# Conv-FFN epilogue in two parts, another order in the pool, first statistics on TensorE

## The chip, the core and the metric

The kernel runs on one core of a Trainium2 chip. The metric is device time in microseconds (us) of one execution; the time of a kernel is the median of its runs. One more execution was taken with the hardware profiler; all rows of the trace are from that one.

## What is computed

One inference step of a trunk of four layers. The input is 128 context tokens and 256 latent tokens, together T = 384 columns of width 1024. Each layer has a token mixer and a Conv-FFN, each behind an RMS norm with shift, scale and gate from the conditioning vector (adaLN):

```python
h = rms_norm(x, g_mix[i]) * (1 + sc1) + sh1
y = chunk_gmlp(h) | multi_pool(h) | attention(h)      # layers 0 and 3 | 1 | 2
x = x + gt1 * y
h = rms_norm(x, g_ffn[i]) * (1 + sc2) + sh2
a, u = jnp.split(h @ w_in, 2, axis=-1)                # 2 x 2816 columns
a = ap[:, :-2] * conv_w[0] + ap[:, 1:-1] * conv_w[1] + ap[:, 2:] * conv_w[2] + conv_b
x = x + gt2 * ((gelu(a) * u) @ w_out)
```

`multi_pool` takes, in four groups of 256 channels, the mean over a window of tokens minus the token itself, and multiplies by a 256 x 256 matrix per group.

## The kernel before

**Layout.** `x` stays in SBUF, transposed: 8 slices of 128 channels by 384 tokens. Every matmul of weights is done in three passes (`mm3`, `vmm`): a weight chunk is split into a rounded part `whi` (ScalarE, line 353) and a remainder `wlo` (VectorE, line 360), the activations likewise (`hh`, `hl`, or `gh`, `gl`), and whi x hi, wlo x hi and whi x lo are added up in PSUM.

**Weights.** All weight chunks (128 x 1024 fp32, 512 KB) stand in one list (`chunk_plan`) in the order of use. `load` issues their transfers on SyncE's queue, at most five ahead of the oldest chunk whose buffer is not free yet. `w_get` hands out the next chunk and splits up to three chunks ahead (four buffers each for `whi` and `wlo`), through `w_split`: first all `whi`, then what the caller gives as `mid`, then `wlo`; only then is the chunk's buffer free for the next transfer. Chunks named `ad` are adaLN weights. They are woven into the list between others (`weave`; `EDGES` says after how many chunks of a phase the first one comes, and how many stand behind the last), and each costs VectorE two products, line 395 (`junk`).

**Order.** Each engine runs its instructions in program order, and that order is written out by hand. So an instruction that waits holds up all that stands behind it on its engine.

**FFN** (`ffn`). The weights of f = 0 and 1 come first (four chunks, `fr`), with the statistics in their midst, then f = 2 to 21, two chunks each (`fi`; in the code kk = 0 and 1, here the halves of f). f fills two PSUM banks, `pa` and `pu`. The pool of banks `mm` has six; f = 3 uses two others. The first NR values of f (3, in layer 1: 4) run on activations that are not yet normed, and their epilogue multiplies by `rbs` first; meanwhile `norm` makes the normed ones. The epilogue of an f is in three parts: `epi_a` (only for f < NR: takes both banks into SBUF), `epi_b` (the convolution: `ab`, `ct`) and `epi_c` (GELU, times u: `gg`); `split_act` then makes `gh` and `gl`. In the first half of f come `epi_a` (as `mid`) and `epi_b` of f - 1 (in the beginning of f - 2), in the second half:

```python
gs = [epi_c(st, t) for st, t in zip(sts, ts)]
w = self.w_get("fi")
for st, g in zip(sts, gs):
    self.split_act(g, gh[st[0]], gl[st[0]])
```

At f = 5 the epilogues of 3 and 4 are done together. For f >= NR `epi_b` reads `pa` and `epi_c` reads `pu` in PSUM.

**Pool** (layer 1). For each of four groups g: `first(g)` multiplies by the group's matrix into two banks; `scaled(g)` takes them into SBUF with the norm's factor `r`; `second(g)` makes the means with the matrices of the windows, for two slices d, each with its residual and the preparation of the next norm (`aft`).

**Head.** `warm` runs matmuls on ones. `x` comes in four transfers. VectorE and ScalarE square and add it up, `first_stats` (in the middle of `a0_mm(0)`) has TensorE add over the channels. `a0_mm(d)` multiplies the conditioning vector with two chunks of adaLN weights for slice d, `a0_fin(d)` turns the result and adds the bias. `diag` and `spread` bring the norm's factor to all partitions, `put` writes the normed slice 0. Then `gmlp` runs over 8 slices k (chunks `gr`, passes of 6 matmuls, line 852), with `a0_fin(k + 1)` behind the first pass and `a0_mm(k + 2)` behind the second.

## Time and profile before

| | |
|---|---|
| median of 3 runs | 1771.77 us (1771.72 to 1775.01) |
| profiled execution | 1772.34 us |
| its span, first to last instruction | 1770.6 us |
| mean granted clock of TensorE | 0.999 |

A row of the trace gives a start and a length in us from the span's start, the engine (PE is TensorE, PEld its weight load, DVE VectorE, ACT ScalarE, SP SyncE), the line of the kernel, what is written from what, and in brackets how long the engine had been idle and what ended that. xN are N instructions put together. An fp32 matmul appears as two instructions.

### The profile page before, as it was taken

The page shows a single profiled execution, that of the slowest core. Times are in us where ns is not written, and L with a number is a line of the kernel's source. Part 1 is how long each engine was busy: PE and PEld are TensorE (multiplying, and loading weights), DVE is VectorE, ACT ScalarE, POOL GpSimd, SP SyncE. Part 2 cuts the span into 40 slices and gives each one's busy share as a digit, 9 for nine tenths or more (in the row PEclk, how much of TensorE's full clock was granted, in tenths as well). Part 3 has the DMA queues.
Part 4 walks back from the last instruction along what each step waited for, and adds up shares of the span by engine and source line. Part 5 has one row for each costly group of instructions (what it writes and reads, how often), then busy time and mean ns, then how long its engine had stood idle before and what let it go on. Part 6 is the DMA issues. An engine that isn't in the chain of part 4 may idle for free.

```text
span 1770.6 us, 26877 instructions
## 1 busy us (share of the span) xinstructions
PE 1748.9 (99%) x10282; PEld 1671.1 (94%) x10282; DVE 1347.4 (76%) x2309; ACT 885.5 (50%) x1661; POOL 3.4 (0%) x32
## 2 busy tenths in 40 slices
PE   9999999999999999999999999999999999999999
PEld 7799899999998999999778999999988999999999
DVE  6888778888986788886787788887775676876632
ACT  4644346444456654532568564553354444754521
POOL 0000000000000000000000000000000000000000
PEclk9999999999999999999999999999999999999999
DMA  9765654565662356566443336556645334354341
GB/s 338 281 220 167 230 196 139 195 199 188 232 219 106 108 190 202 185 226 208 175 150 132 119 132 200 191 173 202 196 166 192 119 132 155 118 180 147 133 155 54
DMA packets 87728, 312.03 MB, mean 176 GB/s; under 512 B 10478, under 2 KB 10990, under 8 KB 87344
## 3 DMA queue, kind: packets, MB, share of 16 engines
q1 hardware_dynamic: 87216, 309.91, 51.4%
q8 instruction: 80, 1.31, 0.3%
q0 software_dynamic: 96, 0.41, 0.1%
q14 instruction: 48, 0.39, 0.1%
q10 hardware_dynamic: 288, 0.01, 0.0%
HBM read 308.45 MB, written 1.84 MB: 175 GB/s over the span
## 4 chain that ended last, share of the span: by engine, by line
PE 79%; DVE 12%; ACT 5%; issue 3%; DMA 2%; ACTq 0%; DVEq 0%; SPq 0%
PE mm L678 60%; PE mm L852 6%; DVE wlo L360 4%; DVE junk L395 4%; ACT whi L353 2%; DMA wraw<-wts 2%; DVE ct L726 2%; PE adaT L678 2%; PE S L678 1%; PE psa L678 1%; PE mm L896 1%; PE S L1133 1%; PE adaT L852 1%; PE psa L852 1%; PE O L1353 0%
## 5 line engine op out<-in xcount | busy, mean ns | idle before, releaser
L678 PE MATMUL mm<-hb,whi 128*128 128x384 f32 (+1 forms) x3936 | 859.2, 337 | 0.0
L678 PEld LDWEIGHTS mm<-hb,whi 128*128 128x128 f32 x3936 | 698.2, 188 | 3.6 <-issue 1.2
L360 DVE TENSOR_TENSOR wlo<-wraw,whi 128x1024 fp32r<-128x1024 f32 (+2 forms) x390 | 466.0, 1201 | 211.7 <-ACT whi L353 211.2
L353 ACT ACTIVATE whi<-wraw 128x1024 fp32r<-128x1024 f32 (+2 forms) x390 | 399.6, 1034 | 252.2 <-PE mm L678 156.1
L678 PE MATMUL mm<-hb,wlo 128*128 128x384 f32 (+1 forms) x1968 | 504.5, 337 | 5.0 <-DVE wlo L360 4.9
L678 PEld LDWEIGHTS mm<-hb,wlo 128*128 128x128 f32 x1968 | 355.9, 188 | 7.8 <-DVE wlo L360 7.8
L395 DVE SCALAR_TENSOR_TENSOR junk<-wraw,condb 128x1024 bf16<-128x1024 f32 x288 | 351.9, 1222 | 7.9 <-ACT condb L1615 2.7
L735 ACT ACTIVATE gg<-ct 128x128 f32<-128x128 f32 (+1 forms) x150 | 46.4, 356 | 245.6 <-DVE ct L726 245.6
L678 PE MATMUL mm<-gh,wlo 128*128 128x384 f32 x448 | 123.3, 336 | 0.6 <-DVE wlo L360 0.6
L678 PE MATMUL mm<-gh,whi 128*128 128x384 f32 x448 | 123.3, 336 | 0.0
L678 PE MATMUL mm<-gl,whi 128*128 128x384 f32 x448 | 123.2, 336 | 0.0
L726 DVE SCALAR_TENSOR_TENSOR ct<-ab,par,ct 128x385 f32<-128x385 f32 x176 | 108.6, 619 | 6.2 <-ACT ct L724 2.5
L852 PE MATMUL mm<-whi,hb 128*128 128x512 f32 x320 | 87.2, 397 | 0.0
L613 ACT ACTIVATE hb<-x,A 128x128 fp32r<-128x128 f32 x96 | 42.5, 455 | 86.1 <-DVE x L468 80.4
L678 PEld LDWEIGHTS mm<-gh,wlo 128*128 128x128 f32 x448 | 81.7, 188 | 1.0 <-DVE wlo L360 1.0
L678 PEld LDWEIGHTS mm<-gh,whi 128*128 128x128 f32 x448 | 81.7, 188 | 0.1
L678 PEld LDWEIGHTS mm<-gl,whi 128*128 128x128 f32 x448 | 81.8, 188 | 0.0
L736 DVE TENSOR_TENSOR gg<-mm,gg 128x384 f32<-128x384 f32 x72 | 40.2, 558 | 47.2 <-ACT gg L735 46.5
L852 PEld LDWEIGHTS mm<-whi,hb 128*128 128x128 f32 x320 | 59.4, 187 | 17.2 <-issue 2.5
L724 ACT ACTIVATE ct<-ab,par 128x385 f32<-128x385 f32 x88 | 62.7, 713 | 3.4
L468 DVE SCALAR_TENSOR_TENSOR x<-mm,prm,x 128x128 f32<-128x128 f32 x92 | 33.6, 411 | 27.0 <-PE mm L678 27.0
L852 PE MATMUL mm<-wlo,hb 128*128 128x512 f32 x160 | 47.0, 399 | 0.0
(291 smaller groups left out, 1769.4 us busy)
## 6 DMA issues: line engine op xcount, KB each, us to landing
wraw<-wts SPq DMA_DIRECT2D x562, 512.0 KB, 3.9
wraw<-wts SPq DMA_DIRECT2D x12, 256.0 KB, 2.9
wraw<-wts SPq DMA_DIRECT2D x8, 384.0 KB, 4.3
x<-x SPq DMA_DIRECT2D x4, 384.0 KB, 4.5
mx<-mix SPq DMA_DIRECT2D x1, 1280.0 KB, 8.3
y<-x SPq DMA_DIRECT2D x3, 384.0 KB, 4.8
condb<-condb SPq DMA_DIRECT2D x1, 1024.0 KB, 6.5
ws<-a_w_s SPq DMA_DIRECT2D x2, 512.0 KB, 5.5
```

The lines of the kernel that those rows point to most:

```text
L353: nc.scalar.activation(hi[:, :n], t[:, :n], AF.Copy)
L360: nc.vector.tensor_tensor(out=lo[:, :n], in0=t[:, :n], in1=hi[:, :n].bitcast(F32), op=ALU.subtract)
L395: nc.vector.scalar_tensor_tensor(out=self.junk.bitcast(BF16), in0=w, scalar=1.0, in1=self.condb[:, c, :], op0=ALU.mult, op1=ALU.mult, accu ...
L468: nc.vector.scalar_tensor_tensor(out=x[:, d, t0:t1], in0=ps[:, t0:t1], scalar=self.prm[:, l, ty * 8 + d, c:c + 1], in1=x[:, d, t0:t1], op0 ...
L613: nc.scalar.activation(self.hh[:, d, t0:t1], self.x[:, d, t0:t1], AF.Copy, scale=A[:, d, c:c + 1])
L678: nc.tensor.matmul(o, w[:, c:c + nw], r, start=(first and p == 0), stop=(last and p == 2))
L724: nc.scalar.activation(t, ab[:, 1:T + 2], AF.Identity, scale=cw[1], bias=cb)
L726: nc.vector.scalar_tensor_tensor(out=t, in0=ab[:, i:i + T + 1], scalar=cw[i], in1=t, op0=ALU.mult, op1=ALU.add)
L735: nc.scalar.activation(g[:, t0:t1], t[:, t0 + c:t1 + c], GELU)
L736: nc.vector.tensor_tensor(out=g, in0=u, in1=g, op=ALU.mult)
L852: nc.tensor.matmul(ps[n][i], hs, w[p == 1][:, c:c + 512], start=(k == 0 and p == 0), stop=(k == 7 and p == 2))
L896: nc.tensor.matmul(ps[:, 128 * i:128 * i + 128], v[:, i, 128 * c:128 * c + 128], ws[:, c // 2, :], start=True, stop=True)
```

## The change

- FFN: the epilogue is one function, `epilogue`, called in both halves of every f. It gets the weights first (both `whi` and `wlo`, with `epi_a` between), then does `epi_c` and `split_act` for what is due, then `epi_b` for the new one, which is due in the next half. From f = 6 on `epi_b` of f - 1 stands in the second half of f, and its `epi_c` in the first half of f + 1. In f = 5 the epilogue of 3 begins in the first half and that of 4 in the second. In layer 1 `norm` takes 2 slices per half instead of 3.
- `EDGES`: in the FFN of layer 1 the first `ad` chunk comes after 12 chunks instead of 8.
- Pool: `first(3)` and `scaled(2)` stand ahead of `second(0)`, `scaled(3)` ahead of `second(1)`; `u` has four buffers instead of three.
- Head: each of the four pieces of `x` is squared (two by ScalarE, two by VectorE, the last in halves) and TensorE adds each up over the channels in its own columns; VectorE sums the five sets. `warm(0)` has 13 matmuls instead of 25, and `warm(1)` comes behind each piece. `a0_mm(0)` stands behind the statistics. The remainder of the first chunk stands behind the first `put`.

```diff
-EDGES = {(0, "gv"): (2, 1), (0, "go"): (5, 0), (3, "gv"): (5, 2), "fi": (8, 2), (3, "go"): (5, 2)}
+EDGES = {(0, "gv"): (2, 1), (0, "go"): (5, 0), (3, "gv"): (5, 2), (1, "fi"): (12, 2), "fi": (8, 2), (3, "go"): (5, 2)}
-WARM = (25, 3, 5)
+WARM = (13, 3, 5)
...
                     if k > stat_k + 1:
                         norm(2)
-            prev = [(0, b[0], b[1]), (1, b[2], b[3])]
+
+            prev, due = [(0, b[0], b[1]), (1, b[2], b[3])], []
+
+            def epilogue(todo, get):
+
+                sts = []
+                w = get(lambda: sts.extend([epi_a(*p) for p in todo]))
+                for st, t in due:
+                    self.split_act(epi_c(st, t), gh[st[0]], gl[st[0]])
+                due[:] = [(st, epi_b(st)) for st in sts]
+                return w
+
             for f in range(2, NF):
                 w0 = TE if f < NR[l] else T
                 pa, pu = (p()[:, :w0] for p in ((self.ps_bank, self.px_bank) if f == 3 else (self.bank, self.bank)))
-                now, prev = (prev, []) if f == 5 else (prev[:1], prev[1:])
                 for kk in range(2):
-                    if kk == 0:
-                        sts = []
-                        w = self.w_get("fi", mid=lambda: sts.extend([epi_a(*p) for p in now]))
-                        ts = [epi_b(st) for st in sts]
-                    else:
-                        gs = [epi_c(st, t) for st, t in zip(sts, ts)]
-                        w = self.w_get("fi")
-                        for st, g in zip(sts, gs):
-                            self.split_act(g, gh[st[0]], gl[st[0]])
+                    todo = [prev.pop(0)] if f < 6 and kk == 0 or f > 4 and kk == 1 else []
+                    w = epilogue(todo, lambda mid: self.w_get("fi", mid=mid))
                     if f < NR[l]:
-                        norm(3)
+                        norm(2 if NR[l] > 3 else 3)
                     for k4 in range(4):
                         k = 4 * kk + k4
                         r = (hh[:, k, :], hl[:, k, :]) if f < NR[l] else (nh[:, k, :], nl[:, k, :])
                         self.mm3([(pa, 256 * k4), (pu, 256 * k4 + 128)], w, r, k == 0, k == 7)
                 prev.append((f, pa, pu))
             assert next(steps, 0) == 0 and len(prev) == 1
-            sts = []
-            self.w_split(self.n_get + 2, lambda: sts.extend([epi_a(*p) for p in prev]))
-            g = epi_c(sts[0], epi_b(sts[0]))
-            self.split_act(g, gh[NF - 1], gl[NF - 1])
+            epilogue(prev, lambda mid: self.w_split(self.n_get + 2, mid))
+            epilogue([], lambda mid: None)
             self.use(1 - self.cur)
             res, after = follow()
             self.out_proj("fo", gh, gl, NF, l, 5, after, mid=self.sqrt_table, after_chunk=1)
...
             def scaled(g):
                 ps = us[g]
-                u = pp.tile([128, 3, 256], F32, tag="u", name="u", bufs=3)
+                u = pp.tile([128, 3, 256], F32, tag="u", name="u", bufs=4)
                 for i in range(3):
                     nc.scalar.activation(u[:, i, :], ps[i // 2][:, 256 * (i % 2):256 * (i % 2) + 256], AF.Copy,
                                          scale=r[:, i:i + 1])
...
             scaled(0)
             first(2)
             scaled(1)
+            first(3)
+            scaled(2)
             second(0)
-            scaled(2)
-            first(3)
+            scaled(3)
             second(1)
-            scaled(3)
             second(2)
             second(3)
             return res
...
         sel = self.cst[:, 512:514]
         rows = {}
-        def a0_mm(d, mid=None):
+        def a0_mm(d):
             if d >= KD:
                 return
             ps = self.ps_bank()[:, 0:256]
...
                     nc.tensor.matmul(ps[j:j + 32, :], self.cond[:, 4 * h + k4, :], w[:, 256 * k4:256 * k4 + 256],
                                      start=(h == 0), stop=(h == 1), skip_group_check=True)
                 self.free(i)
-                if mid is not None:
-                    mid()
-                    mid = None
             rows[d] = self.tmp.tile([128, 256], F32, tag="adarow", name="a0row", bufs=1)
             nc.vector.tensor_copy(rows[d], ps)
...
         nc.scalar.activation(self.cond[:, :, 0:2], cin, AF.Silu)
-        acc = self.new_acc()
         xf = self.x.rearrange("p k t -> p (k t)")
         with self.tc.tile_pool(name="start", bufs=1) as sp:
-            sum2 = sp.tile([128, 2 * T], F32, tag="sum2", name="sum2")
-            nc.vector.tensor_tensor(out=sum2, in0=xf[:, 0:2 * T], in1=xf[:, 0:2 * T], op=ALU.mult)
-            for d in range(2, KD, 2):
-                sq = sp.tile([128, 2 * T], F32, tag="sq2", name="sq2", bufs=3)
-                nc.scalar.activation(sq, xf[:, T * d:T * d + 2 * T], AF.Square)
-                nc.vector.tensor_tensor(out=sum2, in0=sum2, in1=sq, op=ALU.add)
-            nc.vector.tensor_tensor(out=acc, in0=sum2[:, 0:T], in1=sum2[:, T:2 * T], op=ALU.add)
+
+            cs = self.px.tile([128, 5, 3], F32, tag="px", name="cs")
+            for n in range(4):
+                sq = sp.tile([128, 2 * T], F32, tag="sq2", name="sq2", bufs=4)
+                t0 = 2 * T * n
+                if n in (1, 2):
+                    nc.scalar.activation(sq, xf[:, t0:t0 + 2 * T], AF.Square)
+                for c0, c1 in {0: [(0, 2 * T)], 3: [(0, T), (T, 2 * T)]}.get(n, ()):
+                    nc.vector.tensor_tensor(out=sq[:, c0:c1], in0=xf[:, t0 + c0:t0 + c1], in1=xf[:, t0 + c0:t0 + c1],
+                                            op=ALU.mult)
+                for g in ((0,), (1,)) if n == 3 else ((0, 1),):
+                    for i in range(3):
+                        for h in g:
+                            nc.tensor.matmul(cs[:, n + (n == 3 and h), i:i + 1],
+                                             sq[:, T * h + 128 * i:T * h + 128 * i + 128], self.ones[:, 0:1],
+                                             start=(h == g[0]), stop=(h == g[-1]), skip_group_check=True)
+                warm(1)
             self.sqrt_table()
-        r = []
-
-        def first_stats():
-            warm(1)
-            r.append(self.stats(acc))
-
-        a0_mm(0, first_stats)
+        m = self.tmp.tile([128, 3], F32, tag="ms", name="ms", bufs=1)
+        nc.vector.tensor_reduce(out=m, in_=cs.rearrange("p n i -> p i n"), op=ALU.add, axis=AX.X)
+        nc.vector.tensor_scalar(out=m, in0=m, scalar1=1.0 / D, scalar2=EPS, op0=ALU.mult, op1=ALU.add)
+        r = [self.rsqrt(m, [128, 3])]
+        a0_mm(0)
         warm(2)
-        R = []
-        self.w_split(1, lambda: R.append(self.diag(r[0])))
-        A = a0_fin(0)
-        rb = self.spread(R[0], self.bank)
         rbs = self.tmp.tile([128, T], F32, tag="acc", name="rb0", bufs=1)
-        self.put([0], lambda k: A, rb, *self.plain(0), 0)
-        nc.scalar.activation(rbs, rb, AF.Copy)
+
+        def first_put():
+            R = self.diag(r[0])
+            A = a0_fin(0)
+            rb = self.spread(R, self.bank)
+            self.put([0], lambda k: A, rb, *self.plain(0), 0)
+            nc.scalar.activation(rbs, rb, AF.Copy)
+
+        self.w_split(1, first_put)
         a0_mm(1)
         nc.sync.dma_start(self.cst[:, 0:512], a["cst"][:, 0:512])
```

## Rows read from the trace of the kernel before

**Rows 1.** The page: span, and busy time of the engines.

```profile
span 1770.6 us, 26877 instructions
...
PE 1748.9 (99%) x10282; PEld 1671.1 (94%) x10282; DVE 1347.4 (76%) x2309; ACT 885.5 (50%) x1661; POOL 3.4 (0%) x32
```

**Rows 2.** TensorE's waits: total us, times, longest.

```profile
PE mm L678 <- DVE wlo L360: 5.5, 8, 1.0
```

**Rows 3.** The chain that ended last: start us, us.

```profile
1035.05 245.52 PE mm L678 x1416
```

**Rows 4.** Warming matmuls alone in one stretch: PE busy (instructions), PEld, clock, DMA share, GB/s.

```profile
1.05:5.90 4.85, 4.85 (x22) 4.85 (x23) 1.00 0.82 266
```

**Rows 5.** The head in order of time: start us, us.

```profile
10.57 0.73 PE L536 MATMUL cs<-ones,acc 128*128 128x1 f32 x6
...
13.39 0.91 PE L551 MATMUL mm<-R,ones 128*128 128x384 f32 x2
...
15.25 0.64 PE L1545 MATMUL psa<-wraw,cond 128*32 128x256 f32 x8 [0.38 <-DMA wraw<-wts]
...
15.82 1.66 PE L852 MATMUL mm<-whi,hb 128*128 128x512 f32 x6
...
20.43 3.06 PE L852 MATMUL mm<-whi,hb 128*128 128x512 f32 x12
```

**Rows 6.** The page, DMA issues: count, KB, median us to landing.

```profile
wraw<-wts SPq DMA_DIRECT2D x562, 512.0 KB, 3.9
```

**Rows 7.** End of the pool and start of the FFN, in order of time.

```profile
550.92 0.42 PE L1045 MATMUL mm<-ms,us 66*128 66x384 f32 x1 [3.39 <-DVE us L1036]
...
553.01 0.74 DVE L1052 SCALAR_TENSOR_TENSOR x<-mm,pgs,x 128x128 f32<-128x128 f32 x2
...
555.87 0.87 PE L678 MATMUL mm<-hb,wlo 128*128 128x386 f32 x4
...
557.41 0.73 DVE L1052 SCALAR_TENSOR_TENSOR x<-mm,pgs,x 128x128 f32<-128x128 f32 x2
```

**Rows 8.** The same stretch: busy time (instructions) of PE, PEld, DVE, ACT, POOL; clock.

```profile
551.00:560.00 9.00, 9.00 (x42) 8.48 (x43) 7.85 (x22) 5.70 (x13) 0.27 (x6) 0.81 0.00 0
```

**Rows 9.** FFN of layer 0, in order of time: TensorE, then VectorE.

```profile
273.31 0.34 PE L678 MATMUL psa<-hb,whi 128*128 128x384 f32 x1
...
298.84 1.22 DVE L360 TENSOR_TENSOR wlo<-wraw,whi 128x1024 fp32r<-128x1024 f32 x1
299.98 1.22 DVE L395 SCALAR_TENSOR_TENSOR junk<-wraw,condb 128x1024 bf16<-128x1024 f32 x1
...
302.60 2.46 DVE L726 SCALAR_TENSOR_TENSOR ct<-ab,par,ct 128x385 f32<-128x385 f32 x4
...
305.75 0.56 DVE L736 TENSOR_TENSOR gg<-mm,gg 128x384 f32<-128x384 f32 x1 [0.22 <-ACT gg L735]
```

**Rows 10.** ScalarE groups in the FFN of layer 0: busy us, mean ns, idle before.

```profile
L724 ACT ACTIVATE ct<-ab,par 128x385 f32<-128x385 f32 x19 | 13.5, 713 | 0.6
...
L722 ACT ACTIVATE ab<-mm 128x128 f32<-128x128 f32 (+1 forms) x36 | 9.5, 314 | 0.0
L592 ACT ACTIVATE gh<-gg 128x384 fp32r<-128x384 f32 x12 | 6.0, 507 | 0.0
```

**Rows 11.** FFN of layer 1, in order of time: TensorE, VectorE.

```profile
590.38 0.51 PE L678 MATMUL mm<-hb,whi 128*128 128x384 f32 x2
...
613.43 1.22 DVE L360 TENSOR_TENSOR wlo<-wraw,whi 128x1024 fp32r<-128x1024 f32 x1
```

**Rows 12.** FFN of layer 2, in order of time: TensorE, VectorE.

```profile
1026.55 0.34 PE L678 MATMUL psa<-hb,whi 128*128 128x384 f32 x1
...
1052.27 1.22 DVE L360 TENSOR_TENSOR wlo<-wraw,whi 128x1024 fp32r<-128x1024 f32 x1
```

**Rows 13.** FFN of layer 3, in order of time: TensorE, VectorE.

```profile
1517.04 0.34 PE L678 MATMUL psa<-hb,whi 128*128 128x384 f32 x1
...
1540.36 1.22 DVE L360 TENSOR_TENSOR wlo<-wraw,whi 128x1024 fp32r<-128x1024 f32 x1
```

## The prediction, made before the changed kernel ran

> **What bounds the kernel now.** I read the page first. TensorE (PE) is busy for 99% of the span [rows 1], so the time can only move where PE waits, or where PE gets more or less to do. The next view is PE's own waits. Of the waits that this change touches, two stand out [rows 2]: eight times a matmul of the FFN or its projection waits for the remainder `wlo` of its weights, 5.5 us together, and the pool's means wait 3.39 us once for `us` [rows 7]. The FFN waits are a matter of layers 0 and 1: the chain of waits runs through 1416 matmuls of layer 2's FFN without a break, 245.52/1416 = 0.1734 us apart [rows 3]. One weight chunk (24 matmuls) is 4.16 us of PE there, one f 8.33 us. A matmul's record lasts 0.34 us against a spacing of 0.17, so each recorded wait loses some 0.17 us more: the eight are worth 5.5 + 1.4 = 6.9 us.
>
> **Head: +5.2 us.** Removed from VectorE (DVE) are one 768-wide product and the sums; 24 of PE's 50 warming instructions go. Added on PE: squares of each x transfer are multiplied with ones, three pieces of 6 matmuls and a last one of 6. An fp32 matmul of this kind is two instructions; the 6 instructions of today's statistics take 0.73 us, 0.111 apart [rows 5]. So today's 6 become 48, and 24 warming instructions stand between and behind them. PE's queue is in order, and the reading is a sum over it. The first 22 warming instructions need until 5.9, 0.22 apart [rows 4] (twice 0.111: PE is at the lower level, 1.2 GHz, there, though the column has 1.00); the last 4 end at 6.4. By then x's first piece is squared. Three times 12 + 6 instructions: 54 x 0.111 = 6.0, so 12.4; the last 12: 13.7. Today the statistics end on PE at 10.57 + 0.73 = 11.3 [rows 5]. Behind them PE still has, in this order: 6 warming (0.67), the moved `a0_mm(0)` (16 instructions, about 0.58 per 8: 1.15), 10 warming (1.1), two transposed pieces (0.45), the spread (0.9 [rows 5]) and `a0_mm(1)` (1.15): 5.4 us. The first weight product, at 15.82 today [rows 5], starts at 19.1. The DVE path beside it (reduction, root, R) is done near 16.6 and hides under this.
>
> Nothing is won in front of it either. What holds the first product today is the transfer for `a0_mm(1)`: PE waits 0.38 us for `wraw` at 15.25 [rows 5], and these five chunks are asked for without any condition, so they land at the same time afterwards. Moving `wlo` behind the norm therefore saves nothing, and it costs: the chunk's buffer comes free when `wlo` (1.22 us, as in [rows 9]) has run. Now that stands behind the norm. The spread ends on PE at 19.1 - 1.15 = 18.0, the norm's turn through DVE and ACT takes some 2 us (a slice of the pool, with the same kinds of operations, 2.2 [rows 7]), `wlo` 1.2: 21.2. The transfers queued behind that release on SP (the second half for `a0_mm(2)` and those after it) are issued there; 3.9 us later [rows 6] it is 25.1, plus half of `a0_mm(2)` 25.7. The third pass, at 20.43 today [rows 5], is then 5.2 us late. After that PE bounds the phase as it does now, so the delay stays. Bounds: 3.3 us if the transfer is early, 6 if it is slower. The nearest row for the transfer is the median of 562, which I take.
>
> **Pool: -0.5 us.** `first(3)` ahead of the means fills PE while the first `us` are made, and the 3.39 us gap ahead of the last means goes [rows 7]. But what sets the gap's far end is a chain of DVE and ScalarE (ACT): residual, norm input, square, 2.2 us for each of 8 slices (553.01 is the start of the sixth, 557.41 of the eighth [rows 7]). It starts about 1.9 us later now, behind `first(3)`, and makes one interruption (the means of group 3) fewer in its middle. Followed through both queues the sixth residual comes 0.7 us later than today, at 553.7 to 554.45. The FFN's first four accumulators are the banks of slices 2 to 5 then, so its fourth matmul waits for this, and the wlo pass, at 555.87 today [rows 7], starts near 554.7: 1.2 us won. The new gap is as long as the old, in two pieces; behind the old one the clock averaged 0.81 over 9 us [rows 8], a loss of 0.19 x 9 = 1.7 us. It may fall again with one matmul between the pieces (then 0.5 us lost) or not (1.2 won, or 1.4 + 1.7 at most). I take a gain of 0.5; bounds 1.2 lost and 5 won, if the whole wait and its clock go.
>
> **FFN: +9.2 us, and the clock +5.1.** What is removed: `whi` no longer stands behind the GELU on ACT, nor `wlo` behind `gg` on DVE. The waits have that shape: `wlo` waits for `whi`, that stands on ACT behind the GELU, the GELU waits for `ct`, and `ct` stands on DVE behind two adaLN products. I expect 6.1 of the 6.9 us back; one early wait in layer 1 and a short one in layer 0 stay.
>
> What is late next is the epilogue itself, and it holds PSUM banks. For f >= NR `epi_b` and `epi_c` read `pa` and `pu` in PSUM. There are six banks of this pool and f takes two. When f = 7 begins, f = 5 (its `epi_c` comes later in the program) and f = 6 hold four, so 7 must have the two of f = 4, and those come free with `gg` of f = 4. In the old order that is issued in the second half of f = 5; in the new one in the first half of f = 6, one chunk later, behind the splits and adaLN products of that half. PE comes to f = 7 two chunks, 8.3 us, behind that point of the program, where it was three, 12.5. And DVE is late here: the remainder that opens f = 5 in layer 0 starts at 298.84, when PE has been in f = 5 since 273.31 + 16.7 = 290.0 [rows 9], 8.8 us; norm and the long epilogues of the first NR chunks have just run.
>
> So I add up DVE's queue in the new order from the remainder that opens f = 5's first half; layer 0 [rows 9]: it starts at 298.84; 1.14 for it (the next starts at 299.98), 2.62 the adaLN pair, 1.23 the two `ct` of f = 3 (2.46 is four), 1.14 `wlo`, 0.56 `gg`, then ACT: 0.55 `gh`, then two `ab`, 0.31 each, and `ct`, 0.71, less their overlap [rows 10]: 1.27; again DVE: 1.27 `ct` of f = 4, 1.14 `wlo`, 2.45 adaLN, 0.56 `gg`: 13.9 us, so 312.8. f = 3 began on PE at 273.31 [rows 9]; f = 7 is due 4 x 8.33 later, at 306.6. That is a stall of 6.2; handovers overlap by some tenths, so 5.9. Layer 1 [rows 11]: `wlo` at 613.43 comes two adaLN pairs earlier by EDGES (4.9 us), 608.5; the same sum with its wider `gg` is 14.1, so 622.6; f = 4 began at 590.38, f = 7 is due at 590.38 + 25.0 + 1.0 for the early wait: 616.4. Stall 5.9 again. Layer 2 [rows 12]: one adaLN pair in the way instead of two, 1052.27 + 11.3 = 1063.6 against 1026.55 + 33.3 = 1059.9: 3.5. Layer 3 [rows 13]: no pair, 1540.36 + 8.9 = 1549.2 against 1517.04 + 33.3 = 1550.4: none. Together 15.3. After its stall each layer has caught up (two `wlo`, two `ct`, `gg`, `gl` and one adaLN pair are 7.2 us of DVE in each 8.33). Net: 15.3 - 6.1 = +9.2.
>
> The clock: a gap of 3.39 us preceded the fall that cost 1.7 us [rows 7, 8]. Three stalls of at least that length: 3 x 1.7 = 5.1. Bounds: none, and twice as much.
>
> DVE is busy for 76% and ACT for 50% of the span [rows 1], so neither is full. Two rules of the Trainium skill pull apart on that. Its page "Perfetto Trace Analysis", section Optimizing Scalar/DVE Operations, says that breaking up instructions of VectorE and ScalarE can help where they are not saturated yet leave gaps elsewhere; by it the FFN would be 6.9 us faster, the first rival below. The section Optimization Strategy of the same page says that repeated gaps can mean that PSUM is too small for the next tile; that is what I find. No stall of that kind is in the trace of before.
>
> **Sum.** Head 5.2, pool -0.5, FFN 9.2, clock 5.1: +19.0. The profiled execution took 1772.34 us, with 1.7 around its span [rows 1]; the median of the three runs is 0.57 lower. 1771.77 + 19.0 = 1790.8; I say 1790.
>
> **Rivals.** (1) The banks do not bind: DVE reaches f = 4's `gg` six microseconds sooner than I count, before PE needs the bank. It decides at f = 7 of layers 0 to 2. For it: the new order has fewer turns between ACT and DVE. Against it: the queue holds the same work, and the lag of 8.8 us is read from rows 9. Then FFN -6.9, clock 0: 1771.8 + 5.2 - 0.5 - 6.9 = 1769.6, not slower; with the pool's whole wait gone as well 1765. 0.15. (2) The stalls come but the clock stays up, or falls only once: 1786. 0.15. (3) The head's extra PE work hides under the transfers, as PE idles there today by parts of a microsecond: 1786. Against it: PE's queue alone sums to 19.1. 0.08. (4) The pool gains its full 5 us: 1786. 0.05. My own forecast: 0.57, with a range of 1784 to 1797 of its own.
>
> **Range and chances.** Low 1778 takes in (2) to (4) together with smaller stalls; high 1798 takes a second stretch of low clock after one or two stalls. Rival 1 lies outside. What a measurement can tell is about 0.2%, 3.5 us. Faster 0.09 and same 0.06 come from rival 1, slower 0.85 from the rest.
>
> **What would show it.** Head: statistics end on PE near 13.7 and the first product starts near 19. FFN: PE waits for `gg` (DVE) once each in layers 0, 1 and 2, near f = 7, and the waits for `wlo` are nearly gone; the granted clock dips behind them. Pool: the 3.4 us wait is gone, and one of about 2 us twice for `x` stands at the FFN's start. I am wrong if PE runs through f = 7, or the first product starts before 17.

## The result and the profile after

The changed kernel takes 1796.76 us (median of 4 runs, 1795.61 to 1798.34); the kernel before, run beside it, 1773.39 us. The ratio is 1.0132 with an interval of 1.0114 to 1.015: 23.4 us more (20.2 to 26.6). That is slower, as forecast, and inside the range (1778 to 1798), 6.8 us above the predicted 1790.

The page of the changed kernel, the counterpart of [rows 1]: the span is 23.4 us longer, and PE's busy time has grown by only 11.5 us.

```profile
span 1794.0 us, 26933 instructions
...
PE 1760.4 (98%) x10318; PEld 1685.6 (94%) x10318; DVE 1348.4 (75%) x2308; ACT 896.9 (50%) x1660; POOL 3.4 (0%) x32
```

So about half of the loss is idle time of PE. TensorE's waits (total us, times, longest) say which:

```profile
PE mm L678 <- DVE gg L736: 14.1, 3, 5.6
PE mm L678 <- DVE hb L607: 4.6, 1, 4.6
...
PE mm L678 <- DVE wlo L360: 0.9, 1, 0.9
```

The eight waits for `wlo` [rows 2] are one, and the pool's 3.39 us for `us` [rows 7] is gone: both edits do what they say. In their place stand three waits for `gg` and one for line 607, the copy of the shift. Where the time goes shows when the starts of the same matmuls in both traces are subtracted:

| stage | later at its end, us | of this the stage's own |
|---|---|---|
| head, to the third pass of its first product (20.4, now 26.9) | 6.5 | 6.5 |
| mixer of layer 0, to f = 3 (273.3, now 280.9) | 7.6 | 1.1 |
| FFN of layer 0, f = 3 to the projection (434.7, now 447.4) | 12.6 | 5.0 |
| projection and pool, to f = 3 of layer 1 (581.9, now 595.0) | 13.1 | 0.5 |
| FFN of layer 1 (744.8, now 761.9) | 17.1 | 4.0 |
| to f = 3 of layer 2 (1026.6, now 1043.5) | 17.0 | -0.1 |
| FFN of layer 2 (1184.6, now 1208.0) | 23.4 | 6.4 |
| layer 3, to the last matmul (1766.5, now 1789.9) | 23.4 | 0.0 |

The FFN first. PE's f = 7 in layers 0, 1 and 2, from the view in order of time; the number in brackets is the wait in front:

```profile
320.28 0.69 PE L678 MATMUL mm<-hb,whi 128*128 128x384 f32 x1 [5.63 <-DVE gg L736]
320.76 0.84 PE L678 MATMUL mm<-hb,wlo 128*128 128x384 f32 x2
321.40 1.48 PE L678 MATMUL mm<-hb,whi 128*128 128x384 f32 x4
322.68 0.84 PE L678 MATMUL mm<-hb,wlo 128*128 128x384 f32 x2
...
635.30 0.69 PE L678 MATMUL mm<-hb,whi 128*128 128x384 f32 x1 [5.26 <-DVE gg L736]
...
1080.51 0.69 PE L678 MATMUL mm<-hb,whi 128*128 128x384 f32 x1 [3.21 <-DVE gg L736]
```

Counted from start to start, less the usual spacing, the three lose 5.9, 5.4 and 3.5 us. Behind each, PE is at the lower of its two levels: four matmuls take 322.68 - 321.40 = 1.28 us there, 0.32 each, against 0.173 [rows 3]. VectorE's queue ahead of the first of them, the counterpart of the sum over [rows 9]:

```profile
306.52 1.23 DVE L360 TENSOR_TENSOR wlo<-wraw,whi 128x1024 fp32r<-128x1024 f32 x1 [0.39 <-ACT whi L353]
...
310.28 1.27 DVE L726 SCALAR_TENSOR_TENSOR ct<-ab,par,ct 128x385 f32<-128x385 f32 x2
...
312.60 0.55 DVE L736 TENSOR_TENSOR gg<-adaT,gg 128x384 f32<-128x384 f32 x1
...
314.93 1.28 DVE L726 SCALAR_TENSOR_TENSOR ct<-ab,par,ct 128x385 f32<-128x385 f32 x2 [0.63 <-ACT ct L724]
...
319.67 0.55 DVE L736 TENSOR_TENSOR gg<-mm,gg 128x384 f32<-128x384 f32 x1
```

The last row is `gg` of f = 4 (read out of the banks `mm`; that of f = 3 reads the two other banks). From the remainder at 306.52 to its end are 13.7 us. PE's f = 7 was due at 280.9 + 33.3 = 314.2.

The five stretches at the lower level, as the view of windows gives them (busy time and instructions of PE, PEld, DVE, ACT, POOL; clock; DMA share; GB/s). The clock 0.50 is 1.2 GHz:

```profile
11.40:18.20 6.80, 6.80 (x40) 5.31 (x39) 1.15 (x7) 1.15 (x2) 0.00 (x0) 0.50 0.41 156
318.60:325.40 6.80, 5.12 (x16) 5.12 (x17) 5.79 (x10) 3.56 (x6) 0.00 (x0) 0.50 0.58 213
564.40:571.20 6.80, 5.45 (x17) 5.48 (x18) 5.87 (x17) 3.81 (x10) 0.00 (x0) 0.50 0.00 0
632.60:639.40 6.80, 4.09 (x13) 4.10 (x14) 5.75 (x10) 3.68 (x7) 0.00 (x0) 0.50 0.47 170
1079.80:1086.60 6.80, 6.09 (x19) 6.09 (x20) 5.75 (x10) 3.56 (x6) 0.00 (x0) 0.50 0.42 157
```

In the FFN 16, 13 and 19 matmuls fall into one; at 0.32 - 0.173 = 0.147 us more for each that is 2.4, 1.9 and 2.8 us. From 5.9 us on the kernel before has only one such stretch, half as long, within [rows 8] (ahead of 5.9 us its warming runs at the lower level too [rows 4], though the column says 1.00):

```profile
552.10:555.50 3.40, 3.40 (x11) 2.96 (x10) 3.32 (x11) 1.72 (x4) 0.27 (x6) 0.50 0.00 0
```

The head in order of time, beside [rows 5]. Between the rows shown the second lot of sums starts at 7.71, the third at 9.72:

```profile
5.71 1.40 PE L1587 MATMUL cs<-ones,sq 128*128 128x1 f32 x12
6.96 0.91 PE L1530 MATMUL spare<-ones 128*128 128x128 f32 x6
...
12.07 2.56 PE L1587 MATMUL cs<-ones,sq 128*128 128x1 f32 x12
14.49 1.63 PE L1530 MATMUL spare<-ones 128*128 128x128 f32 x6
16.05 1.94 PE L1546 MATMUL psa<-wraw,cond 128*32 128x256 f32 x16
17.91 1.50 PE L1530 MATMUL spare<-ones 128*128 128x128 f32 x10
...
21.44 1.65 PE L853 MATMUL mm<-whi,hb 128*128 128x512 f32 x6
23.87 0.61 PE L1557 MATMUL a0T<-cst,a0row 128*128 128x2 f32 x4 [0.78 <-DVE a0row L1550]
24.34 1.64 PE L853 MATMUL mm<-wlo,hb 128*128 128x512 f32 x6
25.91 1.07 PE L1546 MATMUL psa<-wraw,cond 128*32 128x256 f32 x16
```

The first product starts 5.6 us later than before (15.82), the third pass (26.91) 6.5. `a0_mm(2)` at 25.91 waits for no transfer.

And the start of layer 1's FFN, beside [rows 7], first TensorE, then VectorE:

```profile
565.75 1.62 PE L678 MATMUL mm<-hb,whi 128*128 128x386 f32 x4 [4.62 <-DVE hb L607]
567.17 1.49 PE L678 MATMUL mm<-hb,wlo 128*128 128x386 f32 x4
...
564.78 0.74 DVE L1053 SCALAR_TENSOR_TENSOR x<-mm,pgs,x 128x128 f32<-128x128 f32 x2
565.44 0.17 DVE L607 CAST hb<-prm 128x16 fp32r<-128x16 f32 x1
```

PE has run out of pool work and waits until VectorE, behind the residual of the sixth slice, copies the shift: two of the 386 columns of each of the FFN's first matmuls.

### The profile page after: what moved, and what is told of

Same layout as the page of the kernel before. It is cut to its first block, busy times and chain, and to the rows that moved or that the text cites. A ratio compares the mean times of both kernels' runs of the same rounds, so it can differ in the third digit from the quotient of the medians.

```text
span 1794.0 us, 26933 instructions
## 1 busy us (share of the span) xinstructions
PE 1760.4 (98%) x10318; PEld 1685.6 (94%) x10318; DVE 1348.4 (75%) x2308; ACT 896.9 (50%) x1660; POOL 3.4 (0%) x32
## 4 chain that ended last, share of the span: by engine, by line
PE 84%; DVE 8%; ACT 4%; issue 2%; DMA 2%; DVEq 0%; ACTq 0%; SPq 0%
PE mm L678 66%; PE mm L853 5%; DVE wlo L360 3%; DVE junk L395 2%; DMA wraw<-wts 2%; PE S L678 1%; PE adaT L678 1%; PE mm L897 1%; PE psa L678 1%; ACT whi L353 1%; PE S L1134 1%; PE adaT L853 1%; PE psa L853 1%; PE spare L1530 1%; PE O L1354 0%
## 5 line engine op out<-in xcount | busy, mean ns | idle before, releaser
L678 PEld LDWEIGHTS mm<-hb,whi 128*128 128x128 f32 x3936 | 704.2, 190 | 23.0 <-DVE gg L736 14.9
L678 PEld LDWEIGHTS mm<-hb,wlo 128*128 128x128 f32 x1968 | 359.5, 190 | 1.3 <-DVE wlo L360 1.3
L592 ACT ACTIVATE gh<-gg 128x384 fp32r<-128x384 f32 x56 | 29.4, 526 | 113.8 <-DVE gg L736 91.2
L592 ACT ACTIVATE hb<-gg 128x384 fp32r<-128x384 f32 x48 | 25.2, 526 | 88.4 <-DVE gg L736 59.4
L593 DVE TENSOR_TENSOR gl<-gg,gh 128x384 fp32r<-128x384 f32 x56 | 31.3, 558 | 33.2 <-ACT gh L592 33.2
```

The source lines that it names most:

```text
L592: nc.scalar.activation(hi, src, AF.Copy)
L593: nc.vector.tensor_tensor(out=lo, in0=src, in1=hi.bitcast(F32), op=ALU.subtract)
L678: nc.tensor.matmul(o, w[:, c:c + nw], r, start=(first and p == 0), stop=(last and p == 2))
```

## Experiments

Every run was timed against the kernel before on the same chip. "Profile" is the shift of the last matmul against [rows 1]'s execution, in us; it is one execution, with its own stretches at 1.2 GHz. All runs of the FFN part contain the new entry of `EDGES`.

| run | median us (before) | ratio, interval | profile |
|---|---|---|---|
| FFN alone | 1785.78 (1773.13) | 1.0075, 1.006 to 1.009 | +14.9 |
| FFN, eight banks | 1778.96 (1773.13) | 1.0034, 1.0021 to 1.0047 | +3.6 |
| FFN, early epilogues | 1785.36 (1773.94) | 1.0072, 1.0056 to 1.0088 | +17.9 |
| FFN, early, eight banks | 1775.67 (1773.94) | 1.0009, 0.9999 to 1.0018 | +4.4 |
| FFN, f = 4 back | 1773.63 (1773.51) | 0.9999, 0.9989 to 1.0008 | +0.8 |
| head alone | 1783.23 (1773.13) | 1.0063, 1.0047 to 1.008 | +8.1 |
| head, warming once | 1780.32 (1773.94) | 1.0039, 1.0024 to 1.0053 | +4.7 |
| head, order alone | 1773.69 (1773.51) | 1.0, 0.999 to 1.0009 | +2.7 |
| pool alone | 1774.27 (1773.13) | 1.0009, 0.9999 to 1.0018 | +1.6 |
| pool, early shift | 1773.79 (1773.94) | 1.0002, 0.9993 to 1.0011 | +0.8 |
| lead of 12 alone | 1771.77 (1773.51) | 0.9987, 0.9979 to 0.9996 | -2.8 |
| lead, pool, early shift | 1771.67 (1773.51) | 0.9985, 0.9977 to 0.9994 | -1.1 |

My theory was that of the prediction: the new order makes f = 7 wait for the banks of f = 4, PE's queue makes the head late, and the pool's chain of residuals keeps what the pool gains.

**One part at a time.** The three parts of the diff, each alone: the FFN with the new entry of `EDGES`, the head with the new `WARM`, the pool. (The expectations say slice for f, piece for one of its halves or chunks, and gate for the part `u` that `gg` reads.)

> The FFN part alone (with its lead of 12 pieces for layer 1); head and pool as before. If the FFN part is what costs, the trace of the changed kernel puts 5.0 us on layer 0, 4.0 on layer 1, 6.4 on layer 2 and nothing on layer 3: TensorE stands at slice 7 behind the gelu of slice 4 in three layers, some 14.5 us in all, and the kernel takes 13 to 17 us more than before. Rival: the loss is made in the head and at the pool, and the FFN part does what it says, that is, takes the 6.9 us of old waits for wlo away: 3 to 7 us less than before.

> The head alone (with its 13 and 26 warming matmuls): statistics by TensorE, the rest of the first chunk behind the norm. Theory: the whole shift of the head in the changed kernel, 6.5 us at the third pass of the first product, reaches the end: 6 to 8 us more than before. Rival: the later start is taken up by waits before the first FFN, and 0 to 2 us remain.

> The pool's order alone (fourth group ahead of the means, four buffers u). Theory: what TensorE gains inside the pool it stands again at the start of layer 1's FFN, 4 to 5 us for the copy of the shift of slice 5 and 1 to 2 us for the next weights, and a longer half-clock stretch follows: 0 to 2 us more than before. Rival: the wait at the start of the FFN is one of the changed FFN, not of the pool; with the old FFN code the gain stays, 3 to 5 us less than before.

Measured: 13.3, 11.2 and 1.6 us more (ratio times the time before), together 26.1 against 23.4 for all, which the intervals allow. The FFN alone shifts layers 0, 1 and 2 by 4.3, 4.1 and 6.4 us and has the waits of the whole change to the tenth:

```profile
PE mm L678 <- DVE gg L736: 14.1, 3, 5.6
...
PE mm L678 <- DVE wlo L360: 0.9, 1, 0.9
```

In the head alone the third pass is 6.2 us late and nothing is taken up afterwards. The pool alone keeps the wait for line 607 at 4.6 us with the old FFN, so it belongs to the pool; inside the pool and at its end this trace loses 1.3 us. But the trace of the head alone, with the old pool and its old wait of 3.4 us, loses 1.4 us at the same place: the stretch at 1.2 GHz behind the wait lasts 6.8 us there, as in the pool alone, and 3.4 us before. The same 45 us in the head alone, in the pool alone and in the head with warming once (below), whose stretch is the short one, show it in the clock (0.92, 0.92, 0.96):

```profile
535.00:580.00 45.00, 41.47 (x250) 38.26 (x250) 29.07 (x69) 26.66 (x59) 0.26 (x6) 0.92 0.33 119
535.00:580.00 45.00, 40.40 (x229) 38.57 (x228) 28.93 (x64) 29.19 (x65) 0.27 (x6) 0.92 0.21 69
535.00:580.00 45.00, 41.45 (x249) 38.67 (x249) 29.40 (x68) 28.13 (x62) 0.27 (x6) 0.96 0.31 113
```

So the 1.3 us is not shown to be the pool's own. From the start of layer 0's projection to f = 3 of layer 1 both traces, with stretches of equal length, take 148.5 us; the kernel before takes 147.1. The FFN went as its theory said. In the pool the wait for the copy came and the time (1.6 us) fits, but the 1 to 2 us expected for the next weights did not come, and the longer stretch is not peculiar to the new order. The head took more than the 6 to 8 us expected in the timed runs, 8.1 in the trace, 1.4 of it at the pool; its rival (0 to 2) is out.

**Whose wait is it in the FFN?** First the banks: f = 7 and every fourth f after it use the two banks that f = 3 uses.

```diff
-pa, pu = (p()[:, :w0] for p in ((self.ps_bank, self.px_bank) if f == 3 else (self.bank, self.bank)))
+pa, pu = (p()[:, :w0] for p in ((self.ps_bank, self.px_bank) if f % 4 == 3 else (self.bank, self.bank)))
```

> The FFN part alone, as in e_ffn, but slice 7 accumulates in the two banks that slice 3 uses (eight banks in rotation in place of six with slice 3 apart). Theory of the banks: slice 7 waits only because it takes over the banks of slice 4, whose gate has not been read; with other banks the waits of 5.9, 5.4 and 3.5 us are gone, no half-clock stretch follows them, and the kernel takes 4 to 7 us less than before. Rival: VectorE is simply too late with the epilogues, whatever the banks; TensorE then stands a slice later or at the output projection for much the same time, and the kernel takes 8 to 16 us more than before.

Measured: 6.0 us more than before (3.7 to 8.3), 6.8 less than with the change's banks. All three waits for `gg` are gone, so the banks were their cause. But neither number expected came: layer 0 gains 2.1 us and layer 1 3.5, and both give it back, and more, behind their last f (4.8 and 4.5 us). TensorE's waits, and layer 0's projection in order of time:

```profile
PE mm L678 <- ACT whi L353: 5.5, 2, 3.5
...
PE mm L678 <- DVE wlo L360: 2.3, 4, 0.9
```

```profile
448.57 0.82 PE L678 MATMUL mm<-gh,whi 128*128 128x384 f32 x2 [3.52 <-ACT whi L353]
449.83 1.01 PE L678 MATMUL mm<-gh,wlo 128*128 128x384 f32 x2 [0.44 <-DVE wlo L360]
```

The splits for the projection stand on ScalarE behind the GELU of the last f, and the new order has that half an f later. PE runs at 0.32 us a matmul behind this wait too. So the lag is still there; without the bank it is paid at the end of layers 0 and 1.

Then the lag: each later epilogue is started half an f earlier, at the first half of the next f. Only f = 4 stays where the change has it.

```diff
-todo = [prev.pop(0)] if f < 6 and kk == 0 or f > 4 and kk == 1 else []
+todo = [prev.pop(0)] if kk == 0 or f == 5 else []
```

> The FFN part with its second part and both halves of the epilogues no later than before: the epilogue of every slice from 5 on starts with the first piece of the next slice (only one of the two of slice 5 is moved to the second piece). Banks as in the change. Theory: the change makes VectorE half a slice late, and the stalls at slice 7 come from that lag; with the epilogues half a slice earlier the stalls of 5.9, 5.4 and 3.5 us shrink to under 2 us each and the kernel stands at -4 to +4 us from before. Rival: the gate of slice 4 is too late for slice 7 whatever comes behind it, since its own epilogue is not moved; then some 13 us over before, as with the change's FFN part.

> As the run with the epilogues half a slice earlier, and slice 7 in the banks of slice 3. Theory: with both the bank and the lag at the end of the layer taken away no wait of the FFN is left but what the weights' second halves give (2 us), the 3.7 us for the first pieces of the output projection in layers 0 and 1 are gone, and the kernel takes 3 to 7 us less than before. Rival: the 3.7 us at the output projection come from the split of its pieces, not from the lag; then 3 to 6 us over before, as with the banks alone.

Measured: with the change's banks nothing is gained (12.8 us more; the 17.9 of the trace include two stretches at 1.2 GHz outside the FFN, at 251.7 and 852.5), and the waits for `gg` are the same to the tenth:

```profile
PE mm L678 <- DVE gg L736: 14.1, 3, 5.6
...
PE mm L678 <- DVE wlo L360: 1.0, 1, 1.0
```

So the rival holds, and my theory in that form falls: it is not a lag that builds up over the epilogues, it is the place of f = 4's own. With eight banks as well the waits for `whi` at the projections shrink from 5.5 to 1.2 us (the other 0.5 of the row below stand inside layer 0's FFN), which shows that the late last epilogue made most of them. But the waits for `wlo` come back, and 1.6 us remain (-0.2 to 3.2), where 3 to 7 less were expected:

```profile
PE mm L678 <- DVE wlo L360: 5.2, 7, 1.0
...
PE mm L678 <- ACT whi L353: 1.7, 4, 1.1
```

Last, f = 4 alone goes back: f = 3 and 4 together at the first half of f = 5, as before the change, and each later f at the first half of the next. The change's banks stay, and so do the splits ahead of the next epilogue.

```diff
-todo = [prev.pop(0)] if f < 6 and kk == 0 or f > 4 and kk == 1 else []
+todo = [prev.pop(0) for _ in range(2 if f == 5 else 1)] if kk == 0 else []
```

> The FFN part with both slices 3 and 4 taken up by the epilogue at the first piece of slice 5, as before the change, and each later slice at the first piece of the next; what stays of the part are the splits of gelu's results ahead of the next epilogue and two norms a piece instead of three. Banks as in the change. Theory: the stall at slice 7 comes from slice 4 alone, whose gate the change moves from the second piece of slice 5 to the first of slice 6; with slice 4 back the stalls of 5.9, 5.4 and 3.5 us are gone or under 1 us each, and the kernel stands within 4 us of before. Rival: VectorE is late in any order, since the splits now stand ahead; 4 to 6 us of stalls at slice 7 remain in all, and the kernel takes 5 to 9 us more.

Measured: the time of before, 0.9999 (0.9989 to 1.0008). The waits:

```profile
PE mm L678 <- DVE gg L736: 6.1, 5, 1.8
...
PE mm L678 <- DVE wlo L360: 1.4, 2, 1.0
```

The three long waits are gone and with them the stretches at 1.2 GHz in the FFN. What is left for `gg` is 6.1 us in five short waits. Those at f = 7 are 1.5, 1.1 and 1.5 us, so the theory's "under 1 us each" failed and the rival's 4 us came; the rival's time (5 to 9 us more) did not, as 4.1 us of waits for `wlo` are gone too. So what is left of the FFN part only exchanges one wait for another. It still has the entry of `EDGES` in it, which alone takes 2.3 us off (below); without the entry this FFN would, by that estimate, be some 2 us slower than before. In the trace layer 2, which the entry does not touch, loses 1.8 us.

**What in the head?** The six warming instructions once, behind the last lot of sums, in place of behind each of four.

```diff
-                warm(1)
+            warm(1)
             self.sqrt_table()
```

> The head part with the six warming matmuls once behind the last piece of the sums, in place of behind each of the four. Theory: TensorE's own queue (four pieces of 1.4 us, three lots of warming of 0.9 to 1.6 us between them) makes the sums end at 14.5 us, long after the last square at 9.0 us; without the lots the sums end at 11 to 12 us and the kernel loses 3 to 5 us where the whole head part lost 8. Rival: the lots only fill time in which TensorE waits for the squares, or the clock falls earlier without them and the sums take the time again; the loss stays at 7 to 9 us.

And the kernel before with the change's order alone: its own sums (`sum2`, `acc`, six columns on PE), then root, `a0_mm(0)`, and `first_put` between `whi` and `wlo` of the first chunk.

```diff
-        a0_mm(0, first_stats)
+        warm(1)
+        r = [self.stats(acc)]
+        a0_mm(0)
         warm(2)
...
+        self.w_split(1, first_put)
```

> The kernel before with its own sums of squares (one accumulator, six columns of TensorE), but the change's order behind them: norm first, then the first chunk's product, and the put of slice 0 ahead of wlo. Theory: of the head's 6.5 us at the third pass some 3 come from the order (the first chunk's 16 matmuls and the copy of its row stand between the norm and the put; the second pass waits 0.8 us more) and 3.5 from the sums; this run shows 2 to 4 us at the third pass and at the end. Rival: the order is free, because the norm is on the path either way; under 1 us, and the sums cost all.

Measured: the order is free at the end, 1.0 (0.999 to 1.0009), with 0.6 us at the third pass; its rival holds, and my theory of 2 to 4 us falls. (The profiled execution shows 2.7 us, 1.3 of them at the pool, where the old wait has a stretch of 6.8 us behind it; the ten timed runs do not.) So the sums on TensorE, with the warming between them, cost the head's time. With the warming in one place the 48 instructions of the sums run through:

```profile
5.41 5.42 PE L1586 MATMUL cs<-ones,sq 128*128 128x1 f32 x48
...
17.51 1.65 PE L852 MATMUL mm<-whi,hb 128*128 128x512 f32 x6
...
29.14 0.64 PE L1545 MATMUL psa<-wraw,cond 128*32 128x256 f32 x8 [0.69 <-DMA wraw<-wts]
```

They end at 10.8 instead of 14.6, the first product starts 1.7 us late instead of 5.4 (in the head alone), and the kernel loses 6.9 us (4.3 to 9.4) instead of 11.2. The edit also takes 18 warming instructions away, at 0.125 us each some 2.3 of the 3.8 us; the rest goes with the clock, which falls here too, at 10.75, but behind the sums and for 3.4 us instead of 6.8. The 0.69 at 29.14 is the next in line, the late transfer of weights; with it and a wait of 0.73 us for `v` (ScalarE) at 64.77 the 2.6 us at the third pass become 4.2 by the mixer's projection. The trace bears out the theory of the queue: 4.7 us, of 3 to 5 expected. The timed runs do not decide it, since their interval reaches from the theory's range into the rival's (7 to 9); the profiled execution had a mean granted clock of 0.998, the four others 0.996. Whether the clock in the head falls because of the sums or because the warming ahead of them is half as long (13 matmuls, before 25) was not tried.

**What keeps the pool's gain?** The copy of the shift is moved from slice 5 to slice 1, in the pool alone (in `prep`, a variable in place of the 5).

```diff
-            if d == 5:
+            if d == self.shift_at:
```

> The pool part, and the copies of the shift (hi and lo) made behind slice 1 of the pool's output instead of slice 5, in the pool alone. Theory: TensorE waits 4.6 us at the start of layer 1's FFN for that copy alone; with it early the wait is under 1.5 us and the pool's gain stays: 2 to 5 us less than before. Rival: the output's eight slices, 2.2 us apart on VectorE and ScalarE, set the start of the FFN, the copy only happens to be the last of them; TensorE then waits nearly as long for other tiles of the first slices, and the kernel is within 2 us of before.

Measured: 1.0002 (0.9993 to 1.0011); the rival holds. TensorE starts the FFN at once and is stopped twice, by the residuals that must still read the banks:

```profile
549.06 0.89 PE L679 MATMUL mm<-hb,whi 128*128 128x386 f32 x2
551.73 0.41 PE L679 MATMUL mm<-hb,whi 128*128 128x386 f32 x1 [1.78 <-DVE x L1054]
553.93 0.66 PE L679 MATMUL mm<-hb,whi 128*128 128x386 f32 x1 [1.79 <-DVE x L1054]
```

The two starts are 2.2 us apart, the chain's step per slice [rows 7].

**The entry of `EDGES`.** The kernel before with `(1, "fi"): (12, 2)` and nothing else.

> The kernel before with nothing but the entry that starts the transfers and splits of layer 1's first FFN weights 12 pieces ahead. Theory: layer 1's waits for wlo, 4.0 us in all before, shrink to about 1.1 us as they did in the changed kernel, with no other wait: 2 to 3.5 us less than before. Rival: in the changed kernel they shrank because its FFN ordered the work otherwise, and the lead does nothing: within 1 us of before.

> The lead of 12 for layer 1, the pool part, and the copy of the shift behind slice 1 in the pool; head and FFN as before. Theory: the two gains add up, 2.8 us from the lead and 0.2 us from the pool: 2 to 4 us less than before. Rival: the pool's weights and layer 1's first FFN weights are split at the same time on VectorE and ScalarE, the pool's outputs come later for it, and the sum is at most 1 us less than before.

The words for the entry in these two and in the run of the FFN alone are wrong: it does not start weights earlier, it puts layer 1's first adaLN chunk behind 12 chunks of the phase instead of 8. The first adaLN product (line 395) of that FFN is at 608.73 instead of 599.93 before. Measured: 0.9987 (0.9979 to 0.9996), 2.3 us less; layer 1's FFN takes 2.5 us less. That is the theory's size; the recorded waits of layer 1 for `wlo` shrink less than it said, from 3.1 us in four to 1.7 in three. Of the 2.8 us in the trace 1.0 arise ahead of the place that the entry changes, and 0.7 of the 2.5 are lost again behind the projection, so 1.8 are shown to be its own. With pool and early shift added it is 0.9985 (0.9977 to 0.9994), 2.7 us less: they add as little as they did alone. Both versions beat both kernels, over the kernel before by about as little as can be told from no change. TensorE's waits with the entry alone, against 5.5 us in eight [rows 2]:

```profile
PE mm L678 <- DVE wlo L360: 4.1, 7, 1.0
```

## Why the prediction was right, and where its sizes were off

**FFN: right, place and size.** The stalls at f = 7 were to be 5.9, 5.9, 3.5 us and none in layer 3; they are 5.9, 5.4, 3.5 and none. The sum over VectorE's queue gave 13.9 us from the remainder to `gg` of f = 4; the rows show 13.7. Shown by the runs: the wait is for the banks (gone with other banks), and most of it comes from moving f = 4's epilogue by one half (1.5 us or less when that alone is undone). The waits for `wlo` come back as counted: the three layers cost 15.4 us, the stalls are 14.8 and the clock 7.1 of it, so 6.5 were regained; 6.1 were forecast.

The Trainium skill's page "Perfetto Trace Analysis", section Optimization Strategy, says that the same gap, repeating, can mean that SBUF or PSUM has no room for the next tile. Here the gap comes once in each of three layers, and the run with eight banks bears that reading out. The section Matmul Optimizations of that page of the Trainium skill asks that all eight banks be in use. The run with eight banks has them all in rotation, takes 6.8 us less than with the change's banks and still 6.0 more than before. The measurement decides: more banks moved the lag, they did not remove it.

**Clock: right in kind, too small.** The term was 3 x 1.7 us after the one fall of [rows 8]; it is 2.4 + 1.9 + 2.8 = 7.1. Each stretch lasts 6.8 us, where the one before lasted 3.4, and that the sizes came out so is in part chance: behind the same wait of 3.2 us in layer 2 the run with early epilogues has a stretch of 3.4 us, and its FFN there loses 5.2 us instead of 6.4. One fall was left out altogether, in the head.

**Head: mis-sized, 6.5 us instead of 5.2.** The sum over PE's queue holds until the clock falls at 11.4: last lot of sums at 12.07, forecast 12.4. From there to 19.25 the last lot of sums, 6 warming instructions, `a0_mm(0)` and 10 more of warming take 7.2 us, where 1.3 + 0.7 + 1.15 + 1.1 = 4.2 were counted. Hence the first product at 21.4 and not 19.1. The other step that failed is the transfer behind the late `wlo`: it was to set the third pass at 25.7, but PE's own queue came later still. It only shows when PE is faster, in the run with the warming once. That the order of norm and `wlo` costs something at the end is not borne out: alone it is free within 1.8 us.

**Pool: wrong sign, 1 us.** Forecast was a gain of 0.5 and two pieces of wait for `x`. The FFN waits in one piece, 4.6 us, for the copy of the shift, which I had overlooked. It stands on VectorE right behind the sixth residual, so the end is nearly the one counted; the two waits for `x` are there behind it and appear, 1.8 us each, when the copy is out of the way. The price is the clock: 17 matmuls fall into the stretch at 1.2 GHz now, 11 before. The prediction had a second fall as its worse case, with 0.5 us lost; that size came, but with one wait and one longer stretch. As the old order has that longer stretch in some traces too, the loss is not shown to come from the new order. The pool loses 0.5 us in the trace of the whole change and 1.3 in that of the pool alone, and its timed ratio cannot be told from 1.

**Rivals.** The banks do bind (the FFN part, 6.9 us faster by the first rival, is 13.3 us slower), the clock fell behind all three stalls, the head was not hidden, the pool did not gain 5 us: none held. The terms add up to 6.5 + 0.5 + 15.4 = 22.4; the remaining 1.0 arises in layer 0's mixer. The wait for the statistics there is 1.6 us, 0.6 before and 0.4 to 1.2 in the runs that change one part; what makes it stays open. The misses do not cancel: against the forecast of 19.0 the head gave 1.3 more, the pool 1.0, the clock 2.0, the mixer 1.0 and the FFN 0.9 less, together 4.4, which is why the time lies near the top of the range.

## What to carry to other kernels

When an epilogue is cut in two and its second part moved later, ask which buffer that part frees, and count the queue of the slower engine from there to the moment at which the fast engine wants it back; that sum was right to a few tenths here. Where an engine off the path runs one unit behind, rearranging its queue exchanges one wait for another (`wlo`, `gg`, `whi`): what helped, by some 2 us, was to move other work away from the crowded stretch, the adaLN products in layer 1. A sum that takes VectorE a few wide instructions may be 48 short ones on the engine that sets the end. And before a loss of 1 to 2 us in one trace is put down to an edit, compare the lengths of the stretches at the lower clock.

## What the hardware showed unexpectedly

- The stretches at 1.2 GHz behind a wait differ: 6.8 us long behind waits of 5.63, 5.26, 4.62 and 3.21 us in the changed kernel; 3.4 us (552.10 to 555.50, clock 0.50) behind the 3.39 us of [rows 7]. The length of the wait does not settle it. Behind that wait of 3.4 us, which the ten traces with the old pool share, the stretch is 3.4 us long in six and 6.8 in four; behind the 3.2 us in layer 2 it is 6.8 us in the changed kernel and in the FFN alone and 3.4 with early epilogues.
- Two waits of 1.8 us with one matmul between them (pool, early shift) were followed by 3.4 us at 0.50 as well. Single waits of at most 1.8 us (f = 4 back) left the FFN's clock alone. But with early epilogues the clock was 0.50 from 251.75 to 255.10, behind a single wait of 1.13 us for the statistics of layer 0, where the changed kernel went on at 1.00 behind 1.56 us at the same place.
- The clock fell in the head with no idle time in front of it and none in it. From 5.71 to 11.40 PE was busy all of 5.69 us at clock 1.00, with one-column sums and warming in turn; from 11.40 to 18.20 all of 6.80 us at 0.50. With the warming in one place it fell behind 5.4 us of sums alone, at 10.75. The kernel before, with its warming in one piece, has 1.00 from 5.9 to 30 us.
- A single-column fp32 instruction was hardly cheaper than one with 128 columns: 12 of the sums take 6.96 - 5.71 = 1.25 us, 0.104 each, 6 warming ones 7.71 - 6.96 = 0.75, 0.125 each. From 5.71 to 11.40 the weight loads (PEld) were busy all of 5.69 us too, 52 of them beside 53 matmul instructions; whether they set the price was not tried.
- The time of one kernel's executions goes with the clock they were granted. Of 33 of the kernel before, the three with a mean clock of 1.000 took 1771.1 to 1771.7 us, the three with 0.996 took 1776.3 to 1776.5.
